# Another simulator decides the order of instructions in a float32 encoder layer

## The chip, the cores and the metric

The kernel runs on one core of a Trainium2 chip. A core has a matrix engine (TensorE, PE in the profile, its weight loads shown as PEld), a vector engine (VectorE, DVE), a scalar engine (ScalarE, ACT), a general engine (GpSimd, POOL) and a queue engine (SyncE, SP) that here only issues DMAs. Each engine runs its own list of instructions strictly in the order in which they stand, and waits on semaphores where an instruction needs another engine's or a DMA's result. The metric is the device time of one execution in microseconds.

## The reference, cut to what matters

One layer of a streaming encoder, in float32, on 1024 prompt frames and 64 sample frames (1088 together) of width 1024:

```python
def mixer(xn, conv_prefix, attn_fn, w_in, w_conv, w_conv_out, w_attn_out, w_out):
    proj = xn @ w_in
    cb, cc, ch, q, k, v, ga, gb = jnp.split(proj, splits, axis=-1)
    cv, conv_state = causal_conv(cc * ch, conv_prefix, w_conv)
    ya = (cb * cv) @ w_conv_out
    o, new_k, new_v = attn_fn(heads(q), heads(k), heads(v))
    yb = o.reshape(B, L, ATT_DIM) @ w_attn_out
    merged = jax.nn.sigmoid(ga) * ya + jax.nn.sigmoid(gb) * yb
    return merged @ w_out, conv_state, new_k, new_v
...
x = x + mixer(rmsnorm(x, g_mix), ...)
x = x + (silu(h @ w_ff1) * (h @ w_ff3)) @ w_ff2      # h = rmsnorm(x, g_ffn)
return rmsnorm(x, g_final)
```

The attention has 8 heads of 64. A frame reads its own chunk of 64 frames and the 8 chunks before it, with a bias per head and relative distance.

## The kernel before

Every float32 operand of a product is split into two parts, high and low, and a product is three matmuls (high by high, high by low, low by high). `split` (lines 119 to 122) makes the parts: a copy on ACT (L121), then a subtraction on DVE (L122). Most large products go through `run` (line 218), which does seven half-size products in place of eight; their matmuls are L238.

The stages stand one after the other in the program:

1. Norm of the inputs, transposes to put channels on partitions, and v (`normed`, `turned1`, `v_tile`, matmuls L466 to L468).
2. Twelve units of the input projection (q, k, the convolution's three inputs, a part of gate gb), L238. Their results go to DRAM scratch.
3. Attention, interwoven with the rest of the gate projection. The gate part is 12 products (`GATES`), each of four pieces of 272 frames (`gate`, line 756), and a piece is 24 matmuls (`product`, L300 to L302), so 1152 matmuls in all. A piece is copied out by ACT (L764) and stored by POOL (L765). The attention is a generator, `attention` (line 934): 8 heads of 9 tiles of 128 frames (the ninth is the 64 sample frames), 72 steps. One step does the scores of tile i (`scores`, L856 and L857, two or four matmuls), the softmax (`softmax`: DVE adds the bias and finds the row's extreme in one instruction, L814; ACT does the exponential, L824), the transposes of tile i-2 (`transposed`, L903) with a split of the result, and for every second tile the product with v of tile i-3 (`values`, L928) and `combine`, which adds the halves (ACT L830, DVE L831 and L832) and has SP store the result to `o_d` (L835, L839). Scores and transposes take turns in the two PSUM buffers of the tag `att` (`patt`, bufs=2). `head_load` has SP load q, k, v and the bias of the next head.
4. After the last step the attention's pools are closed. `u` (the convolution's result) and `ob` (the attention's result) take their place in SBUF: SP loads the gates of the first block (`gates_in`), then u (L990), `ob` and the softmax sums `rc` (L993, L997), and per quarter of the channels DVE multiplies (L1000) and a split follows. Two `rc` buffers serve four quarters. The program places this in front of the last three gate products (`LAST = 3`), 288 matmuls.
5. `ya` and `yb`, the two branch products (L300 to L302), weighed by the gates; `w_out` (L1066 to L1071); the second norm.
6. Eleven pairs of feed-forward units (L238, names with a and b), hidden values stored to `h_d` by POOL.
7. The down projection (L1508) with weights `w2r` loaded by SP and kept in a ring, and the final norm.

How gate pieces and attention steps mix is written out: `between` (line 954) advances the attention by 2.7 steps per piece (`PER`).

```python
    def between():
        credit[0] += PER
        while credit[0] >= 1:
            credit[0] -= 1
            next(steps, None)
```

What is written is not yet the order in which an engine runs it. The tile framework records all instructions with their dependencies, and when its context closes it plays them through a simulator of the machine: whenever an engine is free in that simulation it is handed, of the instructions that are ready there, the one that stands earliest in the program. The order so found is the order of that engine's list on the chip. Which instructions are ready at a moment hangs on the simulator's durations.

## Time and profile before

| | |
|---|---|
| median of 3 runs | 1516.06 us (1512.9 to 1516.81) |
| span of the profiled execution, first to last instruction | 1513.8 us |
| PE busy | 1476.9 us, 98% of the span |
| PE weight loads busy | 1381.1 us, 91% |
| DVE busy | 981.2 us, 65% |
| ACT busy | 682.7 us, 45% |
| DMA | 264.73 MB, mean 175 GB/s |

The profiled execution has no time of its own beside its span; the span lies within the three runs, 2.3 us under their median. A matmul in the profile lasts longer than the distance to the next one, because matmuls are pipelined: 24 matmuls of 272 columns follow each other in 3.01 us, though each is shown as 0.29 us long. So busy PE says that PE is never without work, not that it is at its peak, and the rate is read from distances. PEclk is the clock that TensorE was granted, as a share of the full one.

### The profile page before, as it was taken

The numbers are of one execution on the slowest core, as the hardware profiler recorded it, in microseconds if no ns is written. First come the engines' busy times: TensorE is split into PE (matmuls) and PEld (weight loads), VectorE is DVE, ScalarE is ACT, GpSimd is POOL, SyncE is SP. The second block draws the span as 40 slices with busy tenths as digits, with TensorE's granted clock in tenths as the row PEclk, the third lists the DMA queues.
The fourth block names the chain that finished last, engine by engine and source line by source line (L and its number), as shares of the span: only waits on it lengthen the run. The fifth ranks groups of instructions, "written<-read, shape, count | busy, mean of one in ns | idle before, by whom it ended". The sixth has DMA issues, their size and how long they took to land.

```text
span 1513.8 us, 26451 instructions
## 1 busy us (share of the span) xinstructions
PE 1476.9 (98%) x10178; PEld 1381.1 (91%) x10178; DVE 981.2 (65%) x1843; ACT 682.7 (45%) x1397; POOL 128.7 (9%) x236
## 2 busy tenths in 40 slices
PE   7999999999999999999999999999999999999997
PEld 5799999999999999998889999999999998788886
DVE  6886465642776752763489667666666668857576
ACT  6654433333776752542256444444444445402123
POOL 1210010001111121000100011100001011000000
PEclk9999999999999999999999999999999999999999
DMA  7597524168676529554432434443334449667675
GB/s 233 181 305 245 184 78 135 57 187 234 181 186 176 151 82 293 164 167 145 140 126 77 143 134 152 144 148 120 117 142 157 143 177 317 234 221 235 222 259 202
DMA packets 167518, 264.73 MB, mean 175 GB/s; under 512 B 19008, under 2 KB 103168, under 8 KB 167264
## 3 DMA queue, kind: packets, MB, share of 16 engines
q1 hardware_dynamic: 146736, 198.23, 42.2%
q0 software_dynamic: 19504, 62.71, 11.4%
q10 hardware_dynamic: 1152, 2.10, 0.4%
q8 instruction: 80, 1.31, 0.4%
q14 instruction: 46, 0.38, 0.1%
HBM read 171.06 MB, written 91.92 MB: 174 GB/s over the span
## 4 chain that ended last, share of the span: by engine, by line
PE 79%; DMA 8%; DVE 6%; ACT 3%; issue 3%; SPq 1%; POOL 0%; ACTq 0%; POOLq 0%; DVEq 0%
PE Aa L238 9%; PE Ab L238 9%; PE A L1508 7%; PE Da L238 4%; PE Db L238 4%; PE D L1508 3%; PE Bb L238 2%; PE Ba L238 2%; PE B L1508 2%; PE wo L1066 2%; PE wo L1068 2%; PE wo L1067 2%; PE t L903 2%; PE Ak L238 2%; PE g L300 2%
## 5 line engine op out<-in xcount | busy, mean ns | idle before, releaser
L1508 PE MATMUL A<-ring,ht 128*128 128x512 f32 x528 | 126.6, 393 | 3.6 <-ACT acc L1518 1.9
L1508 PEld LDWEIGHTS A<-ring,ht 128*128 128x128 f32 x528 | 98.8, 188 | 27.2 <-ACT acc L1518 3.2
L300 PE MATMUL g<-xn,whp 128*128 128x272 f32 x384 | 113.2, 295 | 0.0
L301 PE MATMUL g<-xn,whp 128*128 128x272 f32 x384 | 112.0, 292 | 0.0
L302 PE MATMUL g<-xn,wlp 128*128 128x272 f32 x384 | 111.6, 291 | 0.0
L121 ACT CAST ring<-w2r 128x512 fp32r<-128x512 f32 (+1 forms) x78 | 43.4, 587 | 105.7 <-PE A L1508 52.6
L121 ACT CAST hq<-sa 128x512 fp32r<-128x512 f32 x77 | 47.7, 619 | 86.4 <-DVE sa L1239 56.6
L814 DVE CUSTOM_DVE_ANT_0 p<-s,bb 128x640 f32<-128x640 f32 (+5 forms) x72 | 47.5, 661 | 45.5 <-DMA bb<-bias_d 28.6
L1227 POOL DMA_DIRECT2D h_d<-hq x77 | 40.9, 532 | 416.5 <-DVE hq L122 242.1
L122 DVE TENSOR_TENSOR hq<-sa,hq 128x512 fp32r<-128x512 f32 x77 | 53.1, 690 | 33.4 <-ACT hq L121 33.3
L300 PEld LDWEIGHTS g<-xn,whp 128*128 128x128 f32 x384 | 72.6, 189 | 1.0
L302 PEld LDWEIGHTS g<-xn,wlp 128*128 128x128 f32 x384 | 72.6, 189 | 0.5
L301 PEld LDWEIGHTS g<-xn,whp 128*128 128x128 f32 x384 | 72.7, 189 | 0.3
L1508 PE MATMUL D<-ring,ht 128*128 128x512 f32 x264 | 63.9, 393 | 1.3 <-ACT acc L1518 1.3
L122 DVE TENSOR_TENSOR wla<-rawa,wha 128x512 fp32r<-128x512 f32 x56 | 38.5, 687 | 40.5 <-ACT wha L121 40.5
L238 PE MATMUL Aa<-tt,wha 128*128 128x272 f32 x352 | 59.1, 289 | 2.5 <-ACT tt L121 2.5
L1508 PEld LDWEIGHTS D<-ring,ht 128*128 128x128 f32 x264 | 49.5, 188 | 13.1 <-ACT acc L1518 1.8
L122 DVE TENSOR_TENSOR ring<-w2r,ring 128x512 fp32r<-128x512 f32 (+1 forms) x78 | 49.0, 647 | 14.4 <-ACT ring L121 14.2
L238 PE MATMUL Ab<-mg,whb 128*128 128x272 f32 x352 | 58.4, 288 | 0.0
L238 PE MATMUL Aa<-mg,wha 128*128 128x272 f32 x352 | 58.3, 288 | 0.0
L238 PE MATMUL Ab<-tt,whb 128*128 128x272 f32 x352 | 58.2, 287 | 0.0
L121 ACT CAST wha<-rawa 128x512 fp32r<-128x512 f32 x56 | 34.8, 621 | 51.3 <-PE Ab L238 35.3
(519 smaller groups left out, 4368.2 us busy)
## 6 DMA issues: line engine op xcount, KB each, us to landing
h_d<-hq POOLq DMA_DIRECT2D x77, 512.0 KB, 3.5
ht<-h_d SPq DMA_DIRECT2D x154, 256.0 KB, 3.7
rawa<-in_w_ff SPq DMA_DIRECT2D x11, 1024.0 KB, 5.9
rawb<-in_w_ff SPq DMA_DIRECT2D x11, 1024.0 KB, 5.4
w2r<-in_w_ff SPq DMA_DIRECT2D x11, 1024.0 KB, 5.8
qd<-q_d SPq DMA_DIRECT2D x32, 272.0 KB, 4.7
rawp<-in_w_in SPq DMA_DIRECT2D x6, 1024.0 KB, 5.9
u_d<-scr SPq DMA_DIRECT2D x8, 544.0 KB, 4.6
```

Source lines behind the costliest of these rows:

```text
L121: act.copy(hi, src)
L122: vec.tensor_tensor(lo, src, hi.bitcast(F32), op=ALU.subtract)
L238: mm(t[:, j, :HN], w[:, k, :], x[p][:, l, k, j * HN : (j + 1) * HN], start=p in (1, 2, 7) and k == 0 and n == 0, stop=k == 3 and n == 2, s ...
L300: mm(out, a, p, start=k == 0, stop=False)
L301: mm(out, a, q, start=False, stop=False)
L302: mm(out, b, p, start=False, stop=k == kt - 1)
L814: vec.tensor_tensor_reduce(out=s if len(ps.shape) == 2 else s.rearrange("p (a b) -> p a b", a=2), in0=ps, in1=bias if len(ps.shape) == 2 e ...
L903: nc.tensor.transpose(tp[:, i * P : (i + 1) * P], s[:, i * P : (i + 1) * P], ident)
L1066: mm(ps, x(k, 0), wh, start=f, stop=False)
L1067: mm(ps, x(k, 0), wl, start=False, stop=False)
L1227: nc.gpsimd.dma_start(h_d[p, c - 1], hq.rearrange("p i l t -> p (i l t)").bitcast(F32))
L1508: mm(t, ht[k][:, j, x], w[:, l], start=p in (1, 2, 7) and k == 0 and n == 0, stop=k == len(ks) - 1 and n == 2, skip_group_check=p in (6, 5 ...
```

## The change

One argument is added where the tile context is made. The framework then plays the instructions through its timeline simulator in place of its default one. What is computed, the tiles, the buffers' numbers and the instructions are the same; the order within each engine's list changes, and with it which semaphore values are waited for.

```diff
@@ -1584,7 +1584,7 @@
         n: nc.dram_tensor(f"in_{n}", a.shape, F32, kind="ExternalInput").ap() for n, a in arrays.items()
     }
     outs = {n: nc.dram_tensor(f"out_{n}", s, F32, kind="ExternalOutput").ap() for n, s, _ in _OUTS}
-    with tile.TileContext(nc) as tc:
+    with tile.TileContext(nc, schedule_with_timeline_sim=True) as tc:
         encoder_kernel(tc, ins, outs)
     r = run_bass_kernel_spmd(nc, [{f"in_{n}": a for n, a in arrays.items()}], core_ids=[0])
     return tuple(r.results[0][f"out_{n}"].reshape(s) for n, _, s in _OUTS)
```

## The prediction

> **What bounds the kernel now.** I read the page first, for the engines' shares, then the table of busy time by stage, then the timeline and the groups of the attention stage, where the change moves most.
>
> ```profile
> span 1513.8 us, 26451 instructions
> PE 1476.9 (98%) x10178; PEld 1381.1 (91%) x10178; DVE 981.2 (65%) x1843; ACT 682.7 (45%) x1397; POOL 128.7 (9%) x236
> PE 79%; DMA 8%; DVE 6%; ACT 3%; issue 3%; SPq 1%; POOL 0%; ACTq 0%; POOLq 0%; DVEq 0%
> ```
>
> PE always has work: 36.9 us of the span (1513.8 - 1476.9) are without any. So an order can win at most about that, and can lose wherever it takes work away that PE now has beside a slow chain. By stage (busy time, count, granted clock, DMA):
>
> ```profile
> 0.00:113.00 113.00, 97.72 (x564) 83.35 (x564) 87.38 (x171) 68.60 (x132) 21.18 (x34) 0.98 0.75 241
> 113.00:343.00 230.00, 229.95 (x1838) 229.13 (x1839) 130.50 (x209) 89.84 (x164) 9.20 (x18) 1.00 0.48 149
> ...
> 363.00:560.00 197.00, 194.15 (x1380) 178.97 (x1379) 138.57 (x330) 136.52 (x321) 32.73 (x62) 0.99 0.59 157
> 560.00:608.00 48.00, 45.44 (x349) 45.00 (x348) 13.39 (x15) 14.24 (x28) 5.95 (x11) 0.96 0.85 266
> ...
> 814.00:1267.00 453.00, 453.00 (x3619) 452.50 (x3618) 310.34 (x521) 203.65 (x386) 44.27 (x83) 1.00 0.41 146
> 1267.00:1300.00 33.00, 28.05 (x118) 21.41 (x117) 26.89 (x46) 17.21 (x32) 2.67 (x5) 1.00 0.91 332
> 1300.00:1514.00 214.00, 205.84 (x907) 168.29 (x906) 140.98 (x256) 57.91 (x118) 0.00 (x0) 0.99 0.68 226
> ```
>
> The unit stages (113 to 343, 814 to 1267) have no idle PE; the start (0 to 113) and the down projection's start (1267 to 1300) have some. The attention (363 to 560) and the stretch behind it (560 to 608) are full only because gate matmuls stand in them.
>
> **The change, part by part.** The built program holds the same 10180 PE instructions, 6659 of them at another place. Counted in the lists, gate matmuls that stand ahead of the scores of a tile (of 1152):
>
> ```
> head, tile     0,0   1,0   2,0   3,0   4,0   4,3   5,0   7,0   7,8
> before         216   288   384   456   528   557   624   768   846
> changed        216   411   635   854  1077  1152  1152  1152  1152
> ```
>
> Before, about 9 gate matmuls go with each step and 306 stay for after the last scores. Changed, 24 go with each step until none is left at head 4, tile 3. The last 33 of the 72 steps, and the loads behind them, then have no gate work beside them. I cost these two, then the rest.
>
> Three terms. First the dense part. A step's own PE time comes from six whole heads before:
>
> ```profile
> 385.22 0.22 PE L856 MATMUL s<-kd,qd 128*128 128x128 f32 x1
> ...
> 526.78 0.22 PE L856 MATMUL s<-kd,qd 128*128 128x128 f32 x1
> 385.20:526.80 141.60, 140.57 (x1005) 129.19 (x1004) 102.87 (x247) 100.16 (x237) 23.22 (x44) 1.00 0.67 177
> 385.20:526.80 141.60, 74.16 (x480) 64.21 (x480) 7.72 (x20) 1.00 0.67 177
> 122.77 3.01 PE Ak L238 x24
> ```
>
> The first rows are the first scores of heads 1 and 7; the fourth is the same window for the gate tiles alone (480 matmuls); the last gives 3.01/24 = 0.125 us per matmul of 272 columns. 141.6 - 480 x 0.125 = 81.6 us for 54 steps, 1.51 us each. The changed dense part is 39 steps x 1.51 + 936 gate matmuls x 0.125 = 176 us, PE-bound as before. No change by itself; the price comes later.
>
> Second, the 33 bare steps. What one takes then is set by the chain through its PSUM buffers and by DVE:
>
> ```profile
> 525.06 0.71 PE L903 MATMUL t<-ident,p 128*128 128x128 f32 x5
> 525.86 0.69 ACT L121 CAST pt<-t 128x640 fp32r<-128x640 f32 x1
> L122 DVE TENSOR_TENSOR pt<-t,pt 128x640 fp32r<-128x640 f32 x32 | 26.2, 820 | 10.8 <-ACT pt L121 10.7
> L814 DVE CUSTOM_DVE_ANT_0 p<-s,bb 128x640 f32<-128x640 f32 x32 | 26.1, 817 | 6.8 <-PE s L857 6.4
> L831 DVE TENSOR_TENSOR ca<-pv,ca 64x512 f32<-64x512 f32 x32 | 21.7, 679 | 5.8 <-ACT ca L830 5.4
> L832 DVE TENSOR_TENSOR co<-ca 64x256 f32<-64x256 f32 x32 | 13.2, 412 | 0.4
> L824 ACT ACTIVATE p<-p,mx 128x640 f32<-128x640 f32 x32 | 26.6, 832 | 1.4 <-DVE mx L814 1.0
> ```
>
> Scores and transposes share two buffers, so the next full-size transposes wait until the last are cast and subtracted: 0.71 + 0.69 + 0.82 us, and three hand-overs of about 0.09 us (525.77 to 525.86) make 2.49 us. In the 1.67 us left, DVE must also fit the reduction (0.82) and, every second step, 0.68 + 0.41, in a fixed order. Following the changed lists from scores 5,6 to 6,2 with these durations I get 14.3 us for five steps, 2.85 each, because a subtraction stands behind a reduction that waits for scores that wait for the subtraction; the small tiles 0 to 3 go at some 2.1. A head's mean is near 2.5 at full clock. Bounds: below, DVE's own work, 102.87/54 = 1.9 us per step (it holds ten weight subtractions, so a little less); above, about 3.6 at half clock throughout. The clock matters:
>
> ```profile
> 366.37:369.79 3.42, 1.72 (x11) 1.19 (x10) 1.44 (x4) 3.41 (x10) 0.00 (x0) 1.00 1.00 292
> 369.79:373.20 3.41, 3.41 (x14) 3.21 (x14) 1.65 (x5) 1.67 (x5) 0.54 (x1) 0.50 1.12 249
> ...
> 598.48:601.90 3.42, 1.32 (x9) 1.05 (x8) 2.58 (x5) 0.69 (x1) 0.00 (x0) 1.00 0.97 328
> 601.90:605.30 3.40, 2.94 (x13) 2.94 (x14) 2.59 (x2) 0.41 (x1) 0.00 (x0) 0.50 0.92 253
> ...
> 1284.50:1287.90 3.40, 1.73 (x7) 1.05 (x6) 3.00 (x5) 2.94 (x6) 0.00 (x0) 1.00 1.06 391
> 1287.90:1291.30 3.40, 2.05 (x9) 1.70 (x10) 3.40 (x8) 1.23 (x3) 0.00 (x0) 1.00 0.30 73
> ```
>
> Where PE was busy for 1.72 or 1.32 of 3.4 us, the next 3.4 us ran at clock 0.50; after 1.73 us they did not. So the edge lies near half idle. A bare step has 1.51 us of PE work in 2.5, 60%: above the edge on average, with single windows below it. I put a good third of the stretch at half clock, where steps go at about 3.3, and take 2.8 us per step. Cost: 33 x (2.8 - 1.51) = 43 us, and about 4 us as the last three tiles drain without cover. Bounds: 33 x (1.9 - 1.51) = 13 to 33 x (3.6 - 1.51) = 69.
>
> The Trainium skill (TensorE: Matmul & The Clock Gate, Part 4: PE-mode transpose) says that transposes do not count as PE work for the clock, and (Part 1) that one mostly idle window halves it. No run here shows the first; by that rule the bare stretch would be cold throughout, the second rival below.
>
> Third, the stretch behind the attention:
>
> ```profile
> 559.62 1.08 SPq L839 DMA_DIRECT2D o_d<-co_s  x2
> ...
> 565.34 3.05 SPq L990 DMA_DIRECT2D u<-u_d  x4
> ...
> 594.17 1.08 SPq L997 DMA_DIRECT2D rc<-rc_d  x2
> DMA to landing us min/median/max: 9.2/12.8/17.3
> 589.89 1.29 DVE L1000 TENSOR_TENSOR rc<-ob,rc 128x1088 f32<-128x1088 f32 x1 [18.73 <-DMA rc<-rc_d]
> 606.45 1.29 DVE L122 TENSOR_TENSOR ob<-rc,ob 128x1088 fp32r<-128x1088 f32 x1 [1.17 <-ACT ob L121]
> ```
>
> From the last store of the attention (559.6) DMA is 0.85 busy (stage row above) with the gates, u, ob and rc; u lands 9 to 17 us after its issue (the landing row is u's), the first quarter of ob is multiplied at 589.9, the third rc load has to wait for a buffer (594.2), and the last quarter is split at 607.7: 48 us. In the changed lists SP has the same loads behind the same last store, so they cannot start earlier. PE has nothing but ya of block 0 (48 matmuls), one piece of ya of block 1 (12) and three quarters of yb (36): 96 x 0.125 = 12 us. I take 1.5 us off the 48 because ACT is free of gate copies. Idle: 46.5 - 12 = 34.5 us, against 2.6 (48.00 - 45.44) idle and 1.7 at half clock before: 30 us, and 2 for the cold restart: 32. Bounds: 20, if these loads ran at the 391 GB/s of the 1284 us window; 36, without overlap of ya.
>
> The rest. In the unit stages matmuls move by up to 72 places between independent banks; PE stays full: 0. SP's head loads and POOL's stores swap places; each head's loads still go out when the buffers of two heads earlier come free, a whole head ahead: 0. At the start the transposes stand further back, and one weight load stands four loads earlier in SP's list:
>
> ```profile
> 54.48 1.06 PE L408 MATMUL xt<-ident,scr 128*128 128x128 f32 x8 [1.71 <-DVE scr L393]
> 1270.45 0.65 SPq L1304 DMA_DIRECT2D w2r<-in_w_ff  x1
> ```
>
> The first can save the 1.71 us and half a cold window, the second up to the 5 us idle between 1267 and 1300; moved DVE work can cost as much. I take -4, between -12 and +6.
>
> Sum: 43 + 4 + 32 - 4 = 75 us on the profiled execution, 1513.8 + 75 = 1589. The median is 2.3 us above that span; since the terms are not known to 2 us, I leave the number at 1589.
>
> **Rivals.** A, bare steps run at DVE's pace: other parts of the attention show fewer waits than my walk. For it: ACT and DVE are 0.73 busy at most in the six heads. Against it: the two PSUM buffers. At 2.0 us: 33 x 0.49 = 16, + 2 + 30 - 6: 1556.
>
> B, the bare stretch stays at half clock.
>
> ```profile
> 603.64 0.23 PE yb L302
> ...
> 606.69 0.13 PE yb L301
> ```
>
> These pieces of the chain of waits show the same matmul at half and at full clock: what lies 0.13 us apart then lies 0.23 apart, the step's PE work becomes some 2.7 us, and the chain about 3.4: 33 x 1.89 = 62, + 5 + 34 - 2: 1613. For it: the idle share is near the edge. Against: at half clock PE is busier than the edge, so it should swing back.
>
> C, not slower. One mechanism: the order removes the idle PE at the other stage borders, some 30 of the 36.9 us. It decides only if the bare steps and the loads cost less than that; at their lowest bounds they cost 13 + 20 = 33, giving 1517. Against it:
>
> ```profile
> 8.25 1.08 PE L408 MATMUL xt<-ident,scr 64*128 64x64 f32 x8 [8.25 <-DVE scr L394]
> ```
>
> 8.25 of those us are the wait for the first input, which no order shortens.
>
> D, the change does nothing: excluded by the lists.
>
> **How the numbers follow.** Main case 0.53 (1589, own range 1570 to 1602), A 0.19, B 0.25, C 0.03. For 8 in 10 the range reaches from A's lower half to a little above B: 1556 to 1622. No change means within 0.3% (4.5 us), about what a measurement of this kernel can tell. Only C is not slower by more: faster 0.01, same 0.02, slower 0.97.
>
> **What would show it.** In the changed profile: no gate matmuls after head 4; PE busy clearly under 90% over some 95 us with steps 2.5 to 3.0 us apart and clock rows of 0.5; then some 30 us of nearly empty PE ahead of yb; the unit stages unchanged. Wrong would be: steps near 2 us or above 3.3, u landing before the last attention store, or yb held by something other than ob.

## The result, and the profile after

The changed kernel takes 1581.02 us (median of four runs, 1575.45 to 1583.03) where the kernel before takes 1515.61 (four runs beside it, 1512.9 to 1516.81): a ratio of 1.0431, 95% interval 1.0411 to 1.0451. It is slower, and the number lies inside the forecast range, 8 us under the forecast. The profiled execution is the fastest of the four (1575.45 us, span 1573.3), so the trace explains 59.5 us (1573.3 - 1513.8), some 6 us less than the medians differ by.

The head of the page, changed kernel:

```profile
span 1573.3 us, 26449 instructions
PE 1486.4 (94%) x10178; PEld 1385.7 (88%) x10178; DVE 982.5 (62%) x1843; ACT 686.0 (44%) x1397; POOL 128.4 (8%) x236
```

Busy PE grew by 9.5 us (1486.4 - 1476.9) though the matmuls are the same: some of them run at half clock. The other 50 of the 59.5 us are time in which PE has nothing. Busy time by stage (stretch, its length, then PE, PE loads, DVE, ACT and POOL, the granted clock, DMA share and GB/s), cut where the changed kernel's stages end:

```profile
113.00:343.00 230.00, 230.00 (x1846) 229.85 (x1845) 134.62 (x215) 93.11 (x169) 9.40 (x18) 1.00 0.49 157
368.20:536.80 168.60, 168.60 (x1294) 164.28 (x1292) 82.61 (x185) 88.15 (x207) 29.35 (x55) 1.00 0.53 151
536.80:615.60 78.80, 59.95 (x342) 44.31 (x341) 62.55 (x150) 56.73 (x131) 8.51 (x17) 0.99 0.48 118
615.60:659.50 43.90, 20.85 (x110) 18.89 (x111) 13.73 (x18) 9.54 (x16) 0.00 (x0) 0.71 0.72 231
...
845.60:906.80 61.20, 49.69 (x372) 49.03 (x371) 47.61 (x84) 30.77 (x59) 1.63 (x3) 0.89 0.19 65
906.80:1284.90 378.10, 378.10 (x3029) 378.10 (x3028) 254.01 (x423) 169.07 (x316) 38.39 (x72) 1.00 0.40 142
```

The rows are: input projection; attention with gates beside it; the 33 bare steps; the loads behind the attention up to the last `yb` of block 0; the second norm, from the last `w_out` product to the end of the first pair of feed-forward units; and the pairs after it but the last. The unit stages have no idle PE, as before. The same points found in the trace of before give, stage by stage:

| from one point to the next | before | after | difference |
|---|---|---|---|
| start to the first scores | 362.9 | 368.2 | +5.3 |
| first scores to the last `yb` of block 0 | 247.0 | 291.3 | +44.2 |
| to the end of the first pair of feed-forward units | 234.8 | 247.3 | +12.5 |
| to the end of the last pair but one | 377.8 | 378.1 | +0.3 |
| to the last matmul | 283.3 | 278.8 | -4.5 |
| to the end of the span | 8.0 | 9.7 | +1.7 |

So three quarters of the loss lie where I looked for them, in the attention and behind it, and the rest at the start, for which I had forecast a gain, and at the second norm, for which I had forecast nothing of its own. What PE waits for, in all (waiting engine and tile, who released it, sum, times, longest):

```profile
PE ya L300 <- DMA u<-u_d: 13.4, 3, 11.9
PE xt L1135 <- DVE some L159: 9.1, 1, 9.1
PE yb L300 <- ACT ob L121: 8.8, 3, 5.9
PE xt L408 <- DVE scr L394: 7.9, 1, 7.9
...
PE xt L408 <- DVE scr L393: 5.1, 1, 5.1
```

The first and the third are the uncovered loads, the second the second norm, the last the first norm; the fourth is the wait for the first input, which the kernel before has too. The bare steps do not appear as one long wait: they are many short ones.

To compare runs in which the gate work lies differently, I count the lost time of a stretch: its length less 1.51 us per step and 0.125 us per gate or branch matmul, the prediction's two prices. Of the 936 gate matmuls behind the first scores, all stand ahead of the last product with v in the changed kernel. Before it is 674: behind that product there are 371 matmuls up to the last `yb` of block 0, and 109 of them are `ya` and `yb` (two more at the edges are counted in the rows below). The two stretches of the kernel before, cut at that product:

```profile
363.00:558.70 195.70, 192.85 (x1371) 177.67 (x1369) 138.07 (x328) 136.25 (x320) 32.28 (x62) 0.99 0.59 157
558.73:609.97 51.24, 48.67 (x372) 48.24 (x373) 14.95 (x20) 15.93 (x31) 6.38 (x12) 0.97 0.80 252
```

| | first scores to last product with v | lost | last product with v to last `yb` | lost |
|---|---|---|---|---|
| before | 195.8 | 2.8 | 51.2 | 4.9 |
| after | 247.3 | 21.6 | 43.9 | 30.3 |

The attention lost 19 us more, the stretch behind it 25 us more: 44.

Inside the bare steps, from the scores of head 4, tile 3 to those of head 7, tile 0 there are 52.45 us for 24 steps, 2.19 us each, at clock 1.00. A piece of the timeline shows what my walk along the lists had right and where it was too slow (start, duration, engine, line, output and input; in brackets the idle time before it and who ended it):

```profile
561.67 0.41 PE L856 MATMUL s<-kd,qd 128*128 128x320 f32 x1 [0.81 <-DVE mx L814]
...
565.07 0.77 PE L903 MATMUL t<-ident,p 128*128 128x128 f32 x5 [0.29 <-DVE pt L122]
...
567.52 0.82 DVE L122 TENSOR_TENSOR pt<-t,pt 128x640 fp32r<-128x640 f32 x1
...
567.62 0.74 PE L903 MATMUL t<-ident,p 128*128 128x128 f32 x5 [1.07 <-ACT pt L121]
...
569.18 0.82 DVE L122 TENSOR_TENSOR pt<-t,pt 128x640 fp32r<-128x640 f32 x1 [0.49 <-ACT pt L121]
...
570.06 0.77 PE L903 MATMUL t<-ident,p 128*128 128x128 f32 x5
...
574.01 0.34 PE L856 MATMUL s<-kd,qd 128*128 128x384 f32 x1
```

The transposes of 565.07 waited for the subtraction (L122) of the tile before them, and those of 570.06 started as soon as the subtraction before them had ended (569.18 + 0.82). From one full-size set of transposes to the next it is 2.55 us (565.07 to 567.62) and 2.44 (567.62 to 570.06), close to the 2.49 us of the round trip through one buffer. The set of 567.62 is the exception: it started 0.1 us after the subtraction of the tile before it had started, and 0.7 us before that ended (567.52 + 0.82). As there are only two buffers, it took the other one, which the scores had left; so the buffers are not always used in turn. The first and the last row are the scores 5,6 and 6,2 of my walk: 12.3 us for the five steps, 2.47 each. The next four steps, up to the scores of head 6, tile 6, take 7.2 us (574.01 to 581.23), 1.80 each.

### The profile page after: what moved, and what is told of

Same layout as the page of the kernel before. It is cut to its first block, busy times and chain, and to the rows that moved or that the text cites. A ratio compares the mean times of both kernels' runs of the same rounds, so it can differ in the third digit from the quotient of the medians.

```text
span 1573.3 us, 26449 instructions
## 1 busy us (share of the span) xinstructions
PE 1486.4 (94%) x10178; PEld 1385.7 (88%) x10178; DVE 982.5 (62%) x1843; ACT 686.0 (44%) x1397; POOL 128.4 (8%) x236
## 5 line engine op out<-in xcount | busy, mean ns | idle before, releaser
L1508 PE MATMUL A<-ring,ht 128*128 128x512 f32 x528 | 130.7, 393 | 2.1 <-DVE acc L1520 1.7
L300 PE MATMUL g<-xn,whp 128*128 128x272 f32 x384 | 111.4, 290 | 0.0
L301 PE MATMUL g<-xn,whp 128*128 128x272 f32 x384 | 111.4, 290 | 0.0
L238 PE MATMUL Aa<-mg,wha 128*128 128x272 f32 x352 | 62.0, 293 | 1.4 <-ACT mg L121 1.4
L122 DVE TENSOR_TENSOR hq<-sa,hq 128x512 fp32r<-128x512 f32 x77 | 52.7, 685 | 15.4 <-ACT hq L121 15.3
L121 ACT CAST whb<-rawb 128x512 fp32r<-128x512 f32 x55 | 34.1, 621 | 63.3 <-PE Aa L238 47.3
L122 DVE TENSOR_TENSOR pt<-t,pt 128x640 fp32r<-128x640 f32 (+2 forms) x64 | 41.9, 654 | 30.9 <-ACT pt L121 30.0
L122 DVE TENSOR_TENSOR wla<-rawa,wha 128x512 fp32r<-128x512 f32 x56 | 38.5, 687 | 33.9 <-ACT wha L121 33.8
```

The costliest lines, as they stand in the source:

```text
L121: act.copy(hi, src)
L122: vec.tensor_tensor(lo, src, hi.bitcast(F32), op=ALU.subtract)
L238: mm(t[:, j, :HN], w[:, k, :], x[p][:, l, k, j * HN : (j + 1) * HN], start=p in (1, 2, 7) and k == 0 and n == 0, stop=k == 3 and n == 2, s ...
L300: mm(out, a, p, start=k == 0, stop=False)
L301: mm(out, a, q, start=False, stop=False)
L1508: mm(t, ht[k][:, j, x], w[:, l], start=p in (1, 2, 7) and k == 0 and n == 0, stop=k == len(ks) - 1 and n == 2, skip_group_check=p in (6, 5 ...
```

## The experiments

### Gate work held back, piece by piece

```diff
-            product(ps[:, :n], gate_w[i], xn, o, n)
+            if anchors[-1] is None:
+                product(ps[:, :n], gate_w[i], xn, o, n)
+            else:
+                with tc.issue_after(anchors[-1]):
+                    product(ps[:, :n], gate_w[i], xn, o, n)
...
     def between():
+        anchors.append(latest[0])
         credit[0] += PER
```

`latest` holds the last matmul of the scores that were traced last.

> The changed kernel, its order of gate pieces against attention steps held back: each piece is issued only after the scores that were traced just before it, so gates reach to the last step (864 of 1152 ahead of the last scores, as in the kernel before). Theory I, the place of the gate work alone costs the 44 us between the first scores and the last yb of block 0: some 44 us less than the changed kernel, so +21 us on the kernel before, with that stretch at about 247 us, no bare steps and no empty TensorE ahead of yb. Theory II, the other new orders inside the attention (SP's loads, POOL's stores, DVE's order) cost a good part: it stays above +35 us. In both, the waits at the start and at the second norm stay.

Measured: 1564.04 us, 1.0318 of before (1.0296 to 1.034), 17 us under the changed kernel where theory I asked for 44.

```profile
371.30:595.40 224.10, 203.86 (x1442) 183.84 (x1440) 138.53 (x329) 140.42 (x323) 33.28 (x63) 1.00 0.51 140
```

The stretch up to the last product with v shrank to 224.1 us and holds 71 gate matmuls more than before (1442 against 1371 in the same stretch), so it lost 22 us (224.1 - 108.7 for the steps - 745 x 0.125), as much as with bare steps. By the numbers theory II stands, but there is another reading: most gate matmuls now come in clumps of 17 to 24 after one step, and the next step or two have nothing between scores and transposes. Before, most of the runs of gate matmuls are two to nine long. The run with eighths, further down, tells the two apart.

### Gates first, with the default simulator

```diff
-PER = 2.7
+PER = 1.0
...
-        if i == len(GATES) - LAST:
-            for _ in steps:
-                pass
-            att_stack.close()
...
         for c in range(4):
             gate(i, (c,))
             between()
+    for _ in steps:
+        pass
+    att_stack.close()
...
```

The lines left out are the pools and the loads of u, ob and rc, which move along.

> The kernel before with the default simulator; the program itself now gives 24 gate matmuls to each step and none to the last 33, and the loads of u, ob and rc stand behind the last gate piece. This is one part of the change done alone. Theory I: +44 us on the kernel before, bare steps 2.1 to 2.2 us apart, 43 to 45 us from the last product with v to the last yb of block 0. Theory II: clearly less than +44, the rest belonging to the timeline simulator's other orders. The start and the second norm should cost nothing here.

Measured: 1570.46 us, 1.0361 (1.0345 to 1.0376), 55 us over the kernel before. Stretches as above, bare and behind:

```profile
533.00:613.60 80.60, 57.59 (x343) 43.69 (x341) 61.54 (x148) 56.41 (x131) 8.52 (x17) 1.00 0.41 112
613.60:660.10 46.50, 20.85 (x110) 19.25 (x111) 14.27 (x19) 9.61 (x16) 0.00 (x0) 0.73 0.70 218
```

These are nearly the changed kernel's rows, made with the default simulator: 295.7 us from the first scores to the last `yb`, +48.6. So the place of the gate work is enough to cost all of the 44, and the timeline simulator's other orders in there cost nothing on top (its own two stretches are 1.8 and 2.6 us shorter). The start (+1.5) and the second norm cost next to nothing here: those losses belong to the timeline simulator.

### Gates spread evenly

Against the run with the gates first:

```diff
-PER = 1.0
+PER = 1.8
```

> As the run with the gates first, but 1.8 steps per gate piece: the gate work reaches evenly to the last step, no step is bare, and none of it is left for the loads behind the attention. Theory I with two terms, bare steps 33 x (2.17 - 1.51) = 22 us and uncovered loads 22 us: only the second is left, +22 us on the kernel before. If the bare steps were the whole cost and the loads hidden: about 0. If the loads were the whole: +44.

Measured: 1547.5 us, 1.0197 (1.0172 to 1.0222), +32 where 22 was expected; 28 of them lie between the first scores and the last `yb` (275.0 against 247.0), the others in ones and twos elsewhere.

```profile
364.60:592.50 227.90, 223.20 (x1634) 209.66 (x1632) 144.64 (x334) 143.11 (x336) 38.10 (x72) 1.00 0.56 152
592.50:639.70 47.20, 20.64 (x110) 18.86 (x111) 14.33 (x19) 9.70 (x16) 0.00 (x0) 0.68 0.68 215
```

All of the attention's work with all gates takes 227.9 us, 2 us over its price (225.7). The changed kernel takes 19.5 us longer for the same work, which is what bare steps cost beside evenly covered ones. The loads without cover lose 34 us here (47.2 - 109 x 0.125) against 4.9 before. Both terms are there, and the uncovered loads are the larger one.

### Three PSUM buffers for the bare steps

Against the run with the gates first:

```diff
-    pmm = pg_stack.enter_context(tc.tile_pool(name="pmm", bufs=3, space=PSUM, reuse_waits="tile"))
+    pmm = pg_stack.enter_context(tc.tile_pool(name="pmm", bufs=1, space=PSUM, reuse_waits="tile"))
...
-    patt = att_stack.enter_context(tc.tile_pool(name="patt", bufs=2, space=PSUM, reuse_waits="tile"))
+    patt = att_stack.enter_context(tc.tile_pool(name="patt", bufs=3, space=PSUM, reuse_waits="tile"))
```

> The run with the gates first, with three PSUM buffers for scores and transposes in place of two, and one for gate pieces in place of three (so the dense part may be slower, and only the 33 bare steps are compared). If the hand-over through two PSUM buffers sets the bare step, it falls from 2.17 us towards the 1.9 us of VectorE's work, and the stretch from the scores of head 4, tile 3 to the last product with v from 79 to about 70 us. If the chain through one tile (bias and extreme, exponential, transposes, split) or VectorE's order sets it, it stays at 2.1 to 2.2.

One run, 1572.09 us. The dense part is slower with one gate buffer; the bare part alone counts. The first row is head 4, tile 3 to head 7, tile 0, the second that up to the last product with v:

```profile
544.55:591.05 46.50, 37.92 (x235) 30.43 (x233) 41.02 (x101) 38.56 (x89) 4.55 (x9) 1.00 0.58 154
544.55:617.60 73.05, 57.38 (x343) 45.31 (x341) 60.49 (x148) 55.62 (x130) 8.52 (x17) 0.97 0.48 124
```

46.5/24 = 1.94 us per step, against 2.23 with two buffers (53.62 us for the same 24) and 2.19 in the changed kernel. DVE is 88% busy (41.02 of 46.5). So with two buffers the hand-over between PE, ACT and DVE through PSUM held the bare step up by some 0.3 us, and with three it is close to DVE's own work: the price of my rival A. The Trainium skill (Perfetto Trace Analysis, Optimization Strategy) says that the same gap, when it keeps returning, can mean too little SBUF or PSUM for the next tile; this pair of runs agrees, with 0.3 us per step.

### Gate work held back in eighths

```diff
-            mm(out, a, p, start=k == 0, stop=False)
-            mm(out, a, q, start=False, stop=False)
-            mm(out, b, p, start=False, stop=k == kt - 1)
+            with tc.issue_after(after[k * len(after) // kt]) if after else ExitStack():
+                mm(out, a, p, start=k == 0, stop=False)
+                mm(out, a, q, start=False, stop=False)
+                mm(out, b, p, start=False, stop=k == kt - 1)
...
+        marks.append(last.ins)
```

`after` holds the scores and transposes of the steps that were traced last.

> The changed kernel with the gate work held back in eighths of a piece: each three matmuls are issued only behind the scores or the transposes of the steps traced last, so some 9 go to each step, as in the kernel before, in place of clumps of 24 in the run with whole pieces held back. Theory I (the place of the gate work costs the 44 us; the clumps cost the 28 us that the attention lost in the run with whole pieces): from the first scores to the last yb of block 0 about 247 us, as before, and about +20 us on the kernel before, all of it at the start and at the second norm. Theory II (other orders of the timeline simulator inside the attention cost those 28 us): the attention stays at 215 us or more up to the last product with v, where the kernel before has 196.

Measured: 1544.28 us, 1.0201 (1.0181 to 1.022): 37 us under the changed kernel.

```profile
371.50:574.50 203.00, 193.84 (x1410) 180.99 (x1408) 138.60 (x328) 135.55 (x320) 33.05 (x63) 1.00 0.57 152
574.50:626.70 52.20, 44.89 (x335) 43.79 (x335) 17.43 (x24) 16.29 (x32) 5.41 (x10) 0.97 0.85 260
```

203.0 us with 39 gate matmuls more than before (1410 - 1371): lost 5 us (203.0 - 108.7 - 713 x 0.125), where before lost 2.8. The whole stretch is 255.2 us, 8 above the 247 that theory I gave; 5 of these are the 39 matmuls (39 x 0.125), which stand in the attention and are missing behind it, where the loads set the end. With the start and the second norm that makes +29 in all, where +20 was expected. So 36 of the 44 us come back by the place of the gate work alone, under the timeline simulator too, and the clumps explain the first run. What the simulator's other orders cost here is at most 3 us in the attention.

### The second norm: three attempts

Held back behind the last normalised row group (`L1125`), on DVE: the preparation of two feed-forward weight groups.

```diff
-    u1.prep(0)
-    u1.prep(1)
+    with tc.issue_after(normed2[0]):
+        u1.prep(0)
+        u1.prep(1)
...
-    for st in range(2, len(STEPS)):
-        u0.prep(st)
+    with tc.issue_after(normed2[0]):
+        for st in range(2, len(STEPS)):
+            u0.prep(st)
```

> The changed kernel with VectorE's share of the feed-forward weights' preparation (two half units of the second, the rest of the first) held back until the last row group of the second norm is done. If that work, put among the norm's short instructions, is what makes TensorE wait 9.1 us for the last transposes and drop to half clock: the stretch from the last w_out product to the first feed-forward product falls from 10.8 us to 1 or 2, the 13 us that this stage lost come back in good part, 6 to 12 us less than the changed kernel. If the norm is late for another reason (its inputs, ScalarE's copies): 0 to 2 us.

Measured: 1581.2 us, 1.0445 (1.0428 to 1.0462): nothing gained. The reason I had gone by are these rows of the changed kernel, from the two row groups ahead of the last one, on DVE:

```profile
843.27 0.15 DVE L155 TENSOR_SCALAR some<-some 128x1 f32<-128x1 f32 x1
843.34 0.69 DVE L122 TENSOR_TENSOR wla<-rawa,wha 128x512 fp32r<-128x512 f32 x1
...
848.15 0.15 DVE L157 RECIPROCAL some<-some 128x1 f32<-128x1 f32 x1
...
854.61 0.15 DVE L159 SCALAR_TENSOR_TENSOR some<-some 128x1 f32<-128x1 f32 x1
```

Each of these two row groups needs some 11 us for its four short instructions on DVE (L155, L157 to L159), with seventeen full-size ones between them, where before a group needs 1.6 to 2.8 us. The last group, for one, before the change:

```profile
800.26 0.15 DVE L155 TENSOR_SCALAR some<-some 128x1 f32<-128x1 f32 x1
...
802.92 0.15 DVE L159 SCALAR_TENSOR_TENSOR some<-some 128x1 f32<-128x1 f32 x1
```

With the weight work held back, the stage from the last `w_out` product on looks like this:

```profile
850.60:913.02 62.42, 54.02 (x374) 52.61 (x373) 49.70 (x87) 30.44 (x59) 1.63 (x3) 0.86 0.19 63
```

The longest wait of PE fell from 9.1 to 4.3 us and its idle time from 11.5 (61.20 - 49.69) to 8.4 us, but more of the stage ran at half clock (mean 0.86, against 0.89), and it took 62.4 us against 61.2.

The same two blocks, held back only behind the last group but one, and on ACT too:

```diff
+    with tc.issue_after(normed2[6]), tc.issue_after(roots[-2]):
```

`roots` holds the norm's square roots on ACT (L156).

> The changed kernel with the same two groups of weight preparation held back, but only until the last row group but one is through the norm, and on ScalarE too. Held back until the very last one, they came too late themselves. If the weight preparation in front of the norm's short instructions is the cause: from the last w_out product to the last product of the first feed-forward unit 61 us becomes 50 to 55 (before: 48), 6 to 10 us less than the changed kernel. If the cause is TensorE's list, in which the transposes of each row group stand one w_out product further back than in the kernel before, with ScalarE's copy of them standing ahead of the next row group's squares: 59 us or more, and no gain.

Measured: 1582.49 us, 1.0425 (1.0405 to 1.0445); the stage took 61.15 us. No gain, as the second theory said. The two row groups now need less than 7 us each on DVE, and PE still waits 4.4 and 3.6 us for row groups. So the weight work among the short instructions is not the cause by itself.

Then PE's list alone, with the transposes of each row group in the place that they have before:

```diff
-            token_product(ps, i, mg_rows(i), KD, lambda k: w2[k])
+            j = ORDER.index(i)
+            for half in (0, 4):
+                at = turned_at.get(j - (3 if half == 0 else 2))
+                with tc.issue_after(at) if at is not None else ExitStack():
+                    token_product(
+                        ps, i, lambda k, l: mg_rows(i)(half + k, l), 4, lambda k: w2[half + k], half == 0, half == 4
+                    )
```

> The changed kernel with TensorE's list alone held to the order of the kernel before at the second norm: the transposes of each row group stand inside the w_out product two groups further on, no longer up to a whole product behind it. Holding back the weight preparation in front of the norm's instructions, on one engine or on two, had not moved this stage (61 to 62 us from the last w_out product to the last product of the first feed-forward unit, before 48). If the late transposes are the cause (ScalarE's copy of them stands ahead of the next group's squares and waits 7.4 us): that stretch falls to 50 to 55 us, 6 to 10 us less than the changed kernel. If it stays above 58 us: the norm's place on VectorE and ScalarE needs more than either, and the cause stays open.

Measured: 1583.14 us, 1.0458 (1.0434 to 1.0481). The first row is the second half of `w_out`, up to its last product, the second the stage that was to shrink:

```profile
746.25:857.60 111.35, 106.00 (x475) 85.70 (x473) 56.12 (x117) 37.77 (x75) 9.24 (x17) 0.97 0.40 131
857.60:912.50 54.90, 48.55 (x366) 47.10 (x365) 42.66 (x74) 27.16 (x51) 1.63 (x3) 0.97 0.19 62
```

The stage did fall to 54.9 us, but the products ahead of it took 111.4 where the changed kernel takes 102.9: the wait moved forward, and from the last `yb` of block 7 to the end of the first pair of units there are 166.3 us, against 164.1 in the changed kernel and 152.0 before. The new lists cost this stage 12 us, and none of the three attempts, on one or two engines' lists, gave them back. Which orders together are the cause stays open.

### The first norm: a place of its own

```diff
-        act.activation(scr[:n, SQ : SQ + D], xt[:n], AF.Square, accum_out=few[:n, :1])
+        act.activation(
+            scr[:n, SQ : SQ + D // 2].bitcast(mybir.dt.bfloat16), xt[:n], AF.Square, accum_out=few[:n, :1]
+        )
...
-            v32 = scr[:, SQ : SQ + ATT]
+            v32 = scr[:, SQ + D // 2 : SQ + D // 2 + ATT]
```

The squares themselves are never read, only their sum is.

> The changed kernel with the squares of the first norm written at half width, so that they no longer share their place in scr with the copy of v that waits to be stored. If the 5.1 us wait of TensorE at 55 to 60 us and the half clock behind it come from that shared place (ScalarE's squares wait for a store to land): first input projection unit 4 to 6 us earlier, 4 to 6 us less than the changed kernel. If the norm's short instructions stand behind weight splits there too: 0 to 2 us.

Measured: 1570.92 us, 1.038 (1.0359 to 1.04): 10 us under the changed kernel. The squares (ACT, L381) in the changed kernel, and then with this edit:

```profile
53.49 1.06 ACT L381 ACTIVATE scr<-scr 128x1024 f32<-128x1024 f32 x1 [0.93 <-DMA out_cache_v_prompt<-scr]
...
55.06 1.05 ACT L381 ACTIVATE scr<-scr 128x1024 f32<-128x1024 f32 x1
```

```profile
46.45 1.06 ACT L381 ACTIVATE scr<-scr 128x1024 bf16<-128x1024 f32 x1
...
49.31 1.06 ACT L381 ACTIVATE scr<-scr 128x1024 bf16<-128x1024 f32 x1 [1.21 <-DMA scr<-in_x_prompt]
```

They no longer stand behind a store on its way to DRAM, run 6 to 7 us earlier, and the first projection unit starts at 74.97 us in place of 82.27. The 5.1 us wait and the half clock behind it are gone. Expected were 4 to 6 us; the first scores come 6.9 us earlier, and the rest of the 10 us between the medians was not followed.

### The second down-projection weights one position earlier, in the kernel before

```diff
-                if first and g == 0 and si == 1:
+                if first and g == 0 and si == 0:
                     W2[nk[1]] = Down(nk[1])
```

> The kernel before with the second weight group of the down projection loaded one position earlier in SP's list, as the timeline simulator's order has it, and nothing else. The changed kernel gained 4.5 us from the last feed-forward product to the end. If that load is the reason: 2 to 4 us less than the kernel before, the idle TensorE in the first third of the down projection mostly gone. If the gain came from elsewhere: within 1 us of it.

Measured: 1514.79 us, 1.0006 (0.9994 to 1.0018): no difference. The waits at the start of the down projection are still there, this one for instance:

```profile
1282.81 1.67 PE L1508 MATMUL A<-ring,ht 128*128 128x512 f32 x6 [2.00 <-ACT acc L1518]
```

Each of them ends with an accumulator (`acc`) being emptied by ACT or DVE, not with weights. The changed kernel's 4.5 us here come from another order of that work or of the matmuls around it; I did not take it apart further.

### Three edits together, and the kernel before with one of them

> The changed kernel with three things at once: gate work held back in eighths, the squares of the first norm in a place of their own, and the weight preparation held back as in the run before. If the three causes are separate and add up: 37 us (gates) and 10 us (start) less than the changed kernel, 1534, and what the second norm gives on top, if anything; some +15 us or less on the kernel before.

Measured: 1535.01 us, 1.0099 (1.0076 to 1.0122), 46 us under the changed kernel; 1534 was expected. The kernel before took 1518.03 us beside this run, 2.4 us more than beside the changed kernel, so the last microseconds of this agreement say little. Gates and start add up; the second norm's edit gave nothing here either (from the last `yb` of block 0 to the end of the first pair of units it takes 248.7 us, before 234.8).

> The kernel before with nothing but the squares of the first norm in a place of their own: an attempt to be faster than both. The run with this on the changed kernel reached the first input projection unit 1.7 us earlier than the kernel before does. If the store of v holds up the default order too (1.7 us of waiting at 53 us and a window at half clock behind it): 2 to 4 us less. If those waits have another reason: within 1 us.

Measured: 1511.01 us against 1518.03 for the kernel before on the same chip, 0.9957 (0.9943 to 0.9971), 7 us or 0.4% faster than before, where 2 to 4 us were expected, and the fastest of all versions. Its start:

```profile
0.00:113.00 113.00, 99.43 (x590) 86.03 (x591) 89.48 (x176) 70.05 (x136) 21.77 (x35) 1.00 0.80 248
```

590 matmuls in place of 564 in the first 113 us, no half-clock window among them, and the first unit at 72.41 us where before has 76.72. The profiled execution is the slowest of this version's six (1514.56 us); it is 5.9 us ahead of the trace of before at the last product with v and gives 3.5 of that back in `w_out`, where 1.9 us of waiting and a half-clock window stand. So the start's part is seen in the trace; the rest of the 7 us was not followed further.

## Why the prediction was right, and where it was not

The forecast was 1589 us for the profiled execution and 1556 to 1622 for the range; the trace gives 1573.3, the median is 1581. The direction, the two main mechanisms and the range were right. The sum was nearer than its terms, and that is partly luck: the bare steps came out 28 us under their term, the loads 6 to 7 us under theirs, and the rest 19 us over its own, with the wrong sign.

- **The dense part**: held. PE is full for 168.6 us up to head 4, tile 3 (176 forecast; the last two tiles' transposes and products fall into the bare part).
- **The bare steps, 43 + 4 us**: the mechanism held in the main, the size did not. The step was put at 2.8 us and measured 2.19, and the term is 19 us of lost time (21.6 - 2.8), or 19.5 against evenly covered steps. The round trip of 2.49 us stands in the trace (2.44 and 2.55 us between full-size transposes), and a third buffer shortened the step. Two other steps of the working failed, by about 0.3 us each. The walk of 14.3 us from scores 5,6 to 6,2 took 12.3, and the small tiles 1.80 us a step where 2.1 was forecast; the walk had every set of transposes wait for the subtraction before it, and that is not always so, as the set of 567.62 shows. How much of the 2 us this explains was not measured. And there was no third of the stretch at half clock: up to head 7, tile 0 the clock stays at 1.00. By the prediction's own test, steps near 2 us, its price was wrong, and rival A's 2.0 us was the better one. A smaller part of the error: the kernel before already lost 2.8 us in the attention, which the comparison of 1.51 with 2.8 left out.
- **The stretch behind the attention, 32 us**: held, with 25 to 26. PE waits 11.9 us for u, then for ob. From the issue of the last store (616.44) to the end of the last split of `ob` (658.16) there are 41.7 us where 46.5 was forecast; from the last product with v to the last `yb` PE is idle for 23 us, at a mean clock of 0.71.
- **The rest, -4 us between -12 and +6**: wrong, +15.3. "At the start the transposes stand further back" and could save 1.71 us: the wait there grew to 5.1 us and brought half clock, because ACT's squares stood behind a store that shares their place; the start lost 5.3 us. The earlier weight load gained nothing by itself, though that stage did become 4.5 us shorter. The second norm has no cost of its own: with "moved DVE work can cost as much" the range of this term ends at +6 us for all these stages together, and this one alone lost 12.5 us. Full-size DVE work does stand there between the short instructions of a chain that PE waits for, but moving it away gained nothing, so the cause of these 12.5 us stays open.
- **Rival B, half clock throughout**: fell. By the rule of the Trainium skill that the full clock does not engage for transposes (TensorE: Matmul & The Clock Gate, Part 4) the bare stretch would have been cold; the trace shows 1.00 (last section). Part 1's rule there, half clock after an idle window, agrees with the stretch behind the attention (0.71): in the changed kernel the 3.4 us from 637.72 have no PE work, and from 641.13 the clock is 0.50.
- **Rival C, not slower**: fell. The down projection's stage became 4.5 us shorter, but idle time grew at the start and at the second norm.
- **What was to be seen**: no gates after head 4, a nearly empty PE ahead of `yb` (23 us without work, 43.9 - 20.85) and unchanged unit stages were there; a mean step of 2.5 to 3.0 us and half-clock rows among the steps were not; the thin stretch is 78.8 us long, not 95.

## What to carry to other kernels

A scheduler that hands an engine whatever is ready first uses up filler work early, and then the slow chains at the end stand bare: count, for each slow stretch, how much independent work the lists leave beside it, and in how fine portions. Before costing a chain through a few buffers, look whether the buffers are given out in turn or to whoever comes. Where a new order has several lists wait for each other, as at the second norm here, expect that holding back one or two of them moves the wait instead of removing it. A scratch place that an outgoing store still reads can hold up an engine that only writes throw-away values there.

## What the runs showed of the hardware that I had not expected

Transposes help to keep the clock up. How much they count for is not shown here: no single weight fits the windows below. The clock changes at the ends of windows of 3.41 us. In windows without transposes the edge lies near 1.55 us of busy PE: 1.55 us was followed by half clock (the faster variant of the kernel before) and 1.58 us was not (the run with the squares moved). Each pair is a window and the one after it:

```profile
695.98:699.40 3.42, 1.55 (x7) 0.97 (x6) 1.03 (x2) 1.06 (x1) 0.00 (x0) 1.00 0.99 239
699.40:702.81 3.41, 3.41 (x9) 2.67 (x8) 0.94 (x2) 0.00 (x0) 1.12 (x2) 0.50 0.39 117
```

```profile
644.66:648.07 3.41, 1.58 (x13) 1.36 (x11) 1.44 (x2) 0.61 (x1) 0.00 (x0) 1.00 0.50 163
648.07:651.49 3.42, 2.03 (x12) 1.60 (x12) 2.55 (x2) 0.80 (x2) 0.00 (x0) 1.00 0.07 22
```

The edge is not sharp: in the two runs with the weight preparation held back there are windows of 1.58 and 1.72 us (from 656.85 in the second attempt, from 659.62 in the first) that were followed by half clock.

In the changed kernel's bare steps a window with 2.31 us of busy PE, 1.47 of it in the transposes' tiles `t` (third row), was not followed by half clock:

```profile
545.56:548.98 3.42, 2.31 (x15) 1.60 (x16) 3.21 (x8) 3.03 (x7) 0.00 (x0) 1.00 0.53 147
548.98:552.39 3.41, 2.73 (x19) 2.24 (x20) 2.74 (x9) 2.67 (x6) 0.00 (x0) 1.00 0.29 78
545.56:548.98 3.42, 1.47 (x10) 1.02 (x10) 0.82 (x1) 0.77 (x2) 1.00 0.53 147
```

Outside `t` it has 0.84 us, far under 1.55; had the transposes not counted, half clock should have followed. Two windows of the run with three PSUM buffers pull in opposite directions. The first, at the start of the kernel, has 1.85 us of busy PE, 1.51 of it in the transposes' tiles `xt` (third row), and the clock stayed; the second has 1.95 us, 1.10 of it in `t` (third row of the second fence), and half clock followed:

```profile
53.55:56.96 3.41, 1.85 (x14) 1.57 (x15) 3.41 (x6) 0.72 (x3) 0.00 (x0) 1.00 0.33 90
56.96:60.38 3.42, 3.42 (x19) 2.88 (x18) 3.02 (x6) 3.29 (x6) 1.70 (x3) 1.00 0.69 226
53.55:56.96 3.41, 1.51 (x13) 1.44 (x14) 0.69 (x1) 0.67 (x2) 1.00 0.33 90
```

```profile
609.92:613.33 3.41, 1.95 (x15) 1.41 (x14) 2.74 (x6) 2.22 (x7) 0.86 (x2) 1.00 0.08 19
613.33:616.74 3.41, 2.02 (x8) 1.53 (x7) 1.32 (x3) 0.78 (x2) 1.13 (x3) 0.50 0.09 21
609.92:613.33 3.41, 1.10 (x10) 0.77 (x9) 1.60 (x3) 0.97 (x3) 1.00 0.08 19
```

With an edge of 1.55, transposes would count for at least 0.8 of their time by the first ((1.55 - 0.34)/1.51) and for less than 0.64 by the second ((1.55 - 0.85)/1.10). So the weight stays open. The ends of PE's records are modelled, and no run was made for it.
